# One output store before a crossbar transpose moves from the sync queue to GpSimd's queue

## The chip, the cores and the metric

The kernel runs on one core of one Trainium2 chip. The metric is the device time of one execution in microseconds. The three runs of the kernel before took 199.21, 198.86 and 199.10 us; their median is 199.1 us. Engines are called as in the profile: PE is TensorE's matmul, PEld its weight load, DVE is VectorE, ACT is ScalarE, POOL is GpSimd, SP is SyncE, which computes nothing and issues transfers. A "q" behind a name (SPq, POOLq) means the queue of that engine.

## The reference

The kernel computes the time-mixing part of an RWKV layer for 16 batches of 2048 tokens with 256 channels, float32 in and out. Each token is mixed with its predecessor by a weight per channel, the mix goes through two projections, one of them through a sigmoid, and the product of both goes through the output projection. The reference also computes a third projection, k, which the output doesn't use.

```python
x_prev[:, 1:, :] = x[:, :-1, :]
xv = x * time_mix_v + x_prev * (1 - time_mix_v)
xr = x * time_mix_r + x_prev * (1 - time_mix_r)
v = xv.reshape(-1, d_model) @ value_weight
r = xr.reshape(-1, d_model) @ receptance_weight
out = (1.0 / (1.0 + np.exp(-r)) * v).reshape(-1, d_model) @ output_weight
```

## The kernel before, in words

**Units.** A batch of 2048 tokens is cut into 4 units of 512 tokens, so there are 64 units (NU), and unit u belongs to batch u // 4. The main loop (line 646) runs once per unit g; its last unit is done by last_unit. The multiplication by time_mix is folded into the weights (w_bf), so mixing is "scale the token by a coefficient, then add its predecessor".

**One step g of the loop**, in the order of the program: TensorE projects unit g with the receptance weight into the accumulator psum_r (project, line 384); ScalarE takes the sigmoid (line 658); transfers and transposes for later units are issued (advance, and the block at line 660); from g=33 on ScalarE copies the output of unit g-2 out of its accumulator and stores it (output, line 471 and store, line 437), earlier steps do this at the end for unit g-1; the mix of coming units is made: VectorE scales one half of the channels (line 354), GpSimd the other half (scale_pool, line 364), from step 34 on ScalarE does some of VectorE's scales (line 638), and VectorE adds the predecessors (add, line 376); TensorE projects the unit with the value weight into psum_v, of which there is one buffer; VectorE multiplies it with the sigmoid into z_sb (line 697); GpSimd's scale for a later pair of units follows. A pair of units shares one scale of GpSimd: the one in step g=39 is for units 42 and 43, first mix, and the one in g=40 is for their second mix. VectorE adds to the first mix of unit 42 right behind the product of g=40, and to its second mix at the start of g=41.

**Two ways to transpose the input.** The projections need channels on the partitions, so the input is transposed. Batches 0 to 9 are loaded as bfloat16 by GpSimd's queue into x_bf and transposed by TensorE (line 272). Batches 10 to 15 (STAGED = 10 and up) go another way: GpSimd's queue loads them, cast to bfloat16, from HBM into a scratch tensor in HBM, x_natural (load, lines 158 and 162), and one DMA transpose by the crossbar for each group of three batches, issued by SP, brings them into xt_both (by_dma, line 254). T_AT = {27: 10, 39: 13} says in which step: batches 10 to 12 in step 27, batches 13 to 15 in step 39. The loads of batches 13, 14 and 15 are issued in steps 33, 34 and 35 (STAGE_AT), held back until the first transpose has landed. Batch 15 is loaded in two halves (HALVED), so loads[15] has two transfers; by_dma waits for the second, called whole in the loop. In by_dma and store, `after=` adds a wait for a transfer to the instruction issued.

**Stores.** The outputs of two units make one store of 1 MB. Stores are issued by SP, in order; some pairs are not stored at once. FIRST = {19: 27, 21: 27, 27: 39} names pairs (by their second unit) that are held until a step with a transpose and stored ahead of it, after the first half of the group's last load (half) has landed. WAITING names pairs that are held until the same step and stored behind the transpose: for step 39, those of units 29, 31, 33 and 35. Step 39 thus has one store ahead of the transpose, that of units 26 and 27, and four behind it. The first five lines of the loop that decide this are:

```python
if g in T_AT:
    half, whole = loads[T_AT[g] + 2]
    for pair in firsts.pop(g):
        store(nc.sync, *pair, after=half)
    last_t = by_dma(T_AT[g], whole)
```

**Queues.** Instructions of one engine run in the order of the program, and an instruction that waits holds up what is behind it on its engine. GpSimd's instructions around step 39 are: the loads of batches 13 to 15 (steps 33 to 35), and one scale of line 364 in each step. SP's are the stores and the transpose.

Of the kernel before, what the change touches and what calls it, by code (L numbers as in the profile page):

```python
# [15 lines left out]
def kernel(  # L16
# [25 lines left out]
    nc = tc.nc  # L42
# [18 lines left out]
    T_AT = {27: 10, 39: 13}  # L61
# [330 lines left out]
    def project_unmixed(ps, mo):  # L392


        parts = [(w_prev[:, ko], ko, 0) for ko in range(KO)]
        parts += [(w_bf[:, 0, ko], ko, 1) for ko in range(KO)]
        for n, (w, ko, lo) in enumerate(parts):
            nc.tensor.matmul(
                out=ps[:, mo, :],
                lhsT=w[:, mo * P : (mo + 1) * P],  # L400
                rhs=xt[0][:, lo : lo + UJ, ko],
                start=(n == 0),
                stop=(n == len(parts) - 1),
            )
# [19 lines left out]
    def store(queue, b, lo, hi, after=None):  # L424
        src = o_sb[b, lo // (2 * UJ)]
        j = lo % (2 * UJ)
        src = src[:, j : j + hi - lo, :]
        if b < STAGED:
            dst = out[b].rearrange("(p j) d -> p j d", p=P)[:, lo:hi, :]
        elif b in STAGED_PAIRS:  # L430
            h = lo // (2 * UJ)
            dst = out[b, h * 2 * TU : (h + 1) * 2 * TU].rearrange("(p j) d -> p j d", p=P)[:, j : j + hi - lo]
        else:
            n = min(hi - lo, UJ)
            dst = out[b, lo * P : hi * P].rearrange("(e p j) d -> p e j d", p=P, j=n)
            src = src.rearrange("p (e j) d -> p e j d", j=n)
        op = queue.dma_start(out=dst, in_=src)
        if after is not None:
            tc.add_manual_dep(op.ins, after.ins.name, SYNC, reason="in turn with the last load")
# [93 lines left out]
    def pieces(g):  # L533

        b, e = divmod(g, UB)
        tile_for(g // 2)
        return [(b, m, e * TU, (e + 1) * TU) for m in range(2)]

    def wrap_slots(piece, one=None, after=None):


        b, _, lo, _ = piece
        by_unit = b < BYUNIT
        key = (b, lo // TU if by_unit else UB - 1)
        if key not in late_copies:
            return
        kos = slice(0, KO) if one is None else slice(one, one + 1)
        if one in (None, KO - 1):
            late_copies.remove(key)
        j = slots(piece).start if by_unit else 0  # L550
        n = UJ if by_unit else J
        if by_unit and j > 0:
            engine = nc.vector if key == (0, 1) else nc.gpsimd
            engine.tensor_copy(out=xt[b][:, j, kos, 0:1], in_=xt[b][:, j - 1, kos, P - 1 : P])
        if key in shifted:
            return
        op = (nc.vector if after is None else nc.gpsimd).tensor_copy(  # L557
            out=xt[b][:, j, kos, 1:P], in_=xt[b][:, j + n, kos, 0 : P - 1]
        )
        if after is not None:  # L560
            tc.add_manual_dep(op.ins, after.ins.name, SYNC, reason="one at a time")
# [4 lines left out]
    def advance(limit):  # L566
        nonlocal tnext
        while tnext <= min(limit, NU - 1):
            b, e = divmod(tnext, UB)
            for n in LOADS.get((b, e), ()):  # L570
                loads[n] = load(n)
            if tnext < NU - BYDMA:
                transposes(tnext)
            tnext += 1
# [71 lines left out]
    for g in range(NU - 1):  # L646
        ps_r = ps_r_pool.tile([P, KO, TU], FP32, name="psum_r")
        if g == 0:
            project_unmixed(ps_r, 0)
            advance(1)  # L650
            project_unmixed(ps_r, 1)
            wrap_slots(pieces(1)[0])
            scale(pieces(1)[0])
            last = add(pieces(1)[0])
        else:
            project(ps_r, g, 0)
        s_sb = zpool.tile([P, KO, TU], BF16, name="s_sb")
        nc.scalar.activation(out=s_sb, in_=ps_r, func=ACT.Sigmoid)  # L658
        advance(START_T[g] if g < len(START_T) else g + LOOK)
        if g in T_AT:  # L660
            half, whole = loads[T_AT[g] + 2]
            for pair in firsts.pop(g):
                store(nc.sync, *pair, after=half)
            last_t = by_dma(T_AT[g], whole)
            for pair in kept.pop(g, []):
                store(nc.sync, *pair)
        if LATE_O < g < NU - 2:
            output(g - 2, z_prev2)
        for p in products.get(g + 1, []):
            if g >= FREE and p[0][1] == 1:  # L670
                scale_act(p[0], (0,))
        for p in [q for q, _ in products[g]] + pooled[g]:
            last_unit_of = p[3] // TU - 1
            need = last_unit_of if p[0] < BYUNIT else min(last_unit_of + 1, UB - 1)
            assert UB * p[0] + need < tnext, (g, p, tnext)
            if g > AHEAD or p not in pooled[g]:
                wrap_slots(p)
        if g == 1:
            load(2)
            scale_act(pieces(2)[1], (1,))  # L680
        for p, kos in products[g]:
            if not (g - 1 >= FREE and p[1] == 1):
                scale(p, kos)
        for p in sums[g]:
            last = add(p)
        for p in pooled[g]:
            if p[0] >= BYUNIT:
                wrap_slots(p)
        ps_v = ps_v_pool.tile([P, KO, TU], FP32, name="psum_v")
        project(ps_v, g, 1)  # L690
        if g == 0:
            scale_act(pieces(1)[1], (0,))
            advance(2)
        z_sb = zpool.tile([P, KO, TU], BF16, name="z_sb")
        n = TU // 2 if g == NU - 2 else TU
        for c in range(0, TU, n):
            nc.vector.tensor_tensor(  # L697
                out=z_sb[:, :, c : c + n],
                in0=s_sb[:, :, c : c + n],
                in1=ps_v[:, :, c : c + n],  # L700
                op=ALU.mult,
            )
        for p in pooled[g]:
            wrap_slots(p, after=last)
            scale_pool(p, last)
        if ZEROS_AT <= g < ZEROS_AT + len(pads):
            zero_rows(*pads[g - ZEROS_AT])
        if g in STAGE_AT:
            b = STAGE_AT[g]
            loads[b] = load(b)  # L710
            for op in loads[b] if b in HALVED else [loads[b]]:
                tc.add_manual_dep(op.ins, last_t.ins.name, SYNC, reason="not beside transposes")
        for p in held[g]:
            add(p)
        if z_prev is not None and not LATE_O <= g < NU - 3:
            output(g - 1, z_prev)
        z_prev2, z_prev = z_prev, z_sb
# [31 lines left out]
```

## Time and profile before

| what | before |
|---|---|
| median of three runs | 199.1 us (198.86 to 199.21) |
| span of the profiled execution | 197.1 us |
| time of the runs outside the span (median less span) | 2.0 us |
| mean granted clock of TensorE | 0.996 |
| HBM read, written | 34.34 MB, 39.90 MB |
| first transpose: issue, landing | 95.38 us, 18.8 us later |
| second transpose: issue, landing | 133.86 us, 15.7 us later |

The profile is of one execution of its own, for which the span is given and no other time. It shows busy time by engine, the chain of work that ended last, groups of instructions by line, and the transfers. In a row of a line, "x1: 333/333/333, 131.3 to 131.3" gives the count, the shortest, median and longest duration in ns, and the first and last start in us. "DMA to landing" is the time from a transfer's issue to its completion. In a timeline a row gives start, duration, engine, line, operation, output<-input, and in brackets the engine's idle time before it with what ended it. In a table of stretches come the stretch, its length, the busy times of PE, PEld, DVE, ACT and POOL with their counts, the granted clock, the busy share of the 16 DMA engines (values over 1 come from overlapping packets) and the GB/s that they moved. Matmul ends are modelled, so neighbouring rows of PE overlap by a little.

### The profile page before, as it was taken

To read this page: it belongs to the slowest core of one execution; us is meant where nothing else is said; L and a number is where in the kernel's file an instruction comes from. 1 tells how busy PE (TensorE), PEld (TensorE's weight loads), DVE (VectorE), ACT (ScalarE), POOL (GpSimd) and SP (SyncE) were. 2 spreads that over 40 slices of the span, in tenths; PEclk is the share of its full clock that TensorE was granted. 3 is DMA by queue.
4 is the path that set the end of the run, shared out by engine and by line. 5 is a ranking of instruction groups with operands and counts; after the bars stand their busy time and mean duration, and the time that the engine had idled before them with its cause. 6 is when DMAs were issued, how large, how long until landed. Compare 5 with 4: busy or idle time off the path is not lost.

```text
span 197.1 us, 3735 instructions
## 1 busy us (share of the span) xinstructions
PE 191.5 (97%) x1358; PEld 123.0 (62%) x1364; DVE 183.1 (93%) x286; ACT 177.1 (90%) x197; POOL 86.3 (44%) x117
## 2 busy tenths in 40 slices
PE   8999999999999999999999999999999999999992
PEld 3556676666666666666666666666666666666660
DVE  0999999999999999999999999999999999999962
ACT  3699899999999999999999999999999999999982
POOL 2845542443665635624334266444433444444200
PEclk9999999999999999999999999999999999999998
DMA  5999999999999999999999999999999999999985
GB/s 185 238 176 224 218 254 262 247 259 262 296 413 283 283 296 332 283 238 198 376 209 290 335 346 186 212 218 241 290 290 419 419 421 419 416 416 421 382 327 221
DMA packets 35593, 58.13 MB, mean 295 GB/s; under 512 B 26004, under 2 KB 27128, under 8 KB 30840
## 3 DMA queue, kind: packets, MB, share of 16 engines
q1 hardware_dynamic: 31792, 41.34, 60.3%
q0 software_dynamic: 3632, 16.44, 41.6%
q8 instruction: 10, 0.16, 0.3%
q10 hardware_dynamic: 152, 0.13, 0.2%
q14 instruction: 7, 0.06, 0.1%
HBM read 34.34 MB, written 39.90 MB: 377 GB/s over the span
## 4 chain that ended last, share of the span: by engine, by line
PE 90%; DMA 6%; POOL 1%; issue 0%; SPq 0%; ACT 0%
PE psum_r L384 27%; PE psum_v L384 27%; PE psum_o L416 27%; PE ps_t L272 8%; DMA x_bf<-in_x_dram 4%; DMA w_f<-n_receptance_weight_dram 2%; PE ps_t L416 1%; POOL x_bf L192 1%; SPq L174 0%; POOL wo_bf L195 0%; PE psum_v L416 0%; POOL x_bf L152 0%; PE ps_t L384 0%; PE psum_r L416 0%; ACT x_bf L446 0%
## 5 line engine op out<-in xcount | busy, mean ns | idle before, releaser
L364 POOL TENSOR_SCALAR mix<-xt_both,c_sb 128x1024 bf16<-128x1024 bf16 (+1 forms) x55 | 61.1, 1110 | 85.5 <-DVE mix L376 82.3
L697 DVE TENSOR_TENSOR z_sb<-s_sb,psum_v 128x1024 bf16<-128x1024 bf16 (+1 forms) x64 | 76.8, 1201 | 2.3 <-PE psum_v L384 1.1
L376 DVE TENSOR_TENSOR mix<-mix,xt_both 128x1024 bf16<-128x1024 bf16 x112 | 76.8, 696 | 1.4
L384 PEld LDWEIGHTS <-w_bf 128*128 128x128 bf16 x512 | 48.5, 98 | 39.2 <-DVE mix L376 0.8
L658 ACT ACTIVATE s_sb<-psum_r 128x1024 bf16<-128x1024 f32 x63 | 65.2, 1034 | 6.2 <-PE psum_r L384 6.0
L384 PE MATMUL psum_v<-mix,w_bf 128*128 128x512 bf16 (+1 forms) x252 | 64.8, 378 | 0.4 <-DVE mix L376 0.2
L384 PE MATMUL psum_r<-mix,w_bf 128*128 128x512 bf16 x250 | 64.6, 379 | 0.2
L416 PE MATMUL psum_o<-wo_bf,z_sb 128*128 128x256 bf16 x486 | 63.2, 273 | 0.0
L416 PEld LDWEIGHTS <-z_sb 128*128 128x128 bf16 x512 | 52.0, 103 | 17.9 <-DVE z_sb L510 0.7
L471 ACT COPY o_sb<-psum_o 128x1024 f32<-128x1024 f32 x50 | 51.2, 1023 | 5.0 <-PE psum_o L416 4.8
L289 ACT COPY xt_both<-ps_t 128x1024 bf16<-128x1024 bf16 x32 | 32.9, 1039 | 0.0
L272 PEld LDWEIGHTS <-x_bf 128*128 128x128 bf16 x304 | 19.8, 98 | 8.4 <-DMA x_bf<-in_x_dram 0.4
L272 PE MATMUL ps_t<-ident,x_bf 128*128 128x128 bf16 x304 | 22.7, 219 | 0.2 <-DMA x_bf<-in_x_dram 0.2
L354 DVE TENSOR_SCALAR mix<-xt_both,c_sb 128x1024 bf16<-128x1024 bf16 (+1 forms) x47 | 21.3, 463 | 0.0
L638 ACT ACTIVATE mix<-xt_both,c_sb 128x1024 bf16<-128x1024 bf16 x14 | 16.3, 1163 | 0.0
L376 DVE TENSOR_TENSOR mix<-mix,xt_first 128x1024 bf16<-128x1024 bf16 x15 | 10.5, 708 | 0.1
L471 ACT COPY x_bf<-psum_o 128x1024 f32<-128x1024 f32 x10 | 10.2, 1015 | 0.0
L354 DVE TENSOR_SCALAR mix<-xt_first,c_sb 128x512 bf16<-128x512 bf16 x22 | 6.6, 350 | 0.3 <-ACT xt_first L282 0.2
L289 ACT COPY xt_first<-ps_t 128x1024 bf16<-128x1024 bf16 x6 | 6.0, 1022 | 0.0
L557 POOL COPY xt_first<-xt_first 128x254 bf16<-128x254 bf16 x5 | 2.0, 392 | 7.2 <-DVE mix L376 7.2
L162 POOL DMA_DIRECT2D x_bf<-in_x_dram x8 | 4.7, 584 | 0.0
L364 POOL TENSOR_SCALAR mix<-xt_first,c_sb 128x512 bf16<-128x512 bf16 x6 | 4.1, 685 | 1.3 <-DVE mix L376 0.8
(68 smaller groups left out, 52.3 us busy)
## 6 DMA issues: line engine op xcount, KB each, us to landing
out_dram<-o_sb SPq DMA_DIRECT2D x25, 1024.0 KB, 12.1
x_bf<-in_x_dram POOLq DMA_DIRECT2D x8, 1024.0 KB, 15.8
x_natural<-in_x_dram POOLq DMA_DIRECT2D x4, 1024.0 KB, 11.8
out_dram<-x_bf SPq DMA_DIRECT2D x4, 1024.0 KB, 14.4
x_natural<-in_x_dram POOLq DMA_DIRECT2D x4, 512.0 KB, 12.7
out_dram<-x_bf SPq DMA_DIRECT2D x4, 512.0 KB, 4.7
x_bf<-in_x_dram POOLq DMA_DIRECT2D x6, 256.0 KB, 7.0
o_sb<-in_x_dram SPq DMA_DIRECT2D x4, 256.0 KB, 3.9
```

What stands on the lines that cost most here:

```text
L162: return nc.gpsimd.dma_start(out=x_bf[b], in_=rows(b), max_dma_last_dim=run)
L272: nc.tensor.transpose(out=ps[:, jj], in_=src[:, jj, ko * P : (ko + 1) * P], identity=idn)
L289: nc.scalar.copy(out=xt[b][:, j0 : j0 + UJ], in_=ps)
L354: nc.vector.tensor_scalar(out=mixed(piece, ko), in0=tokens(piece, 0, ko), scalar1=c_sb[:, m, ko : ko + 1], scalar2=None, op0=ALU.mult,)
L364: op = nc.gpsimd.tensor_scalar(out=mixed(piece, 1), in0=tokens(piece, 0, 1), scalar1=c_sb[:, m, 1:2], scalar2=1.0, op0=ALU.mult, op1=ALU.mult,
L376: return nc.vector.tensor_tensor(out=mixed(piece), in0=mixed(piece), in1=tokens(piece, 1), op=ALU.add)
L384: nc.tensor.matmul(out=ps[:, mo, :], lhsT=w_bf[:, m, ko, mo * P : (mo + 1) * P], rhs=mixed((b, m, e * TU + lo, e * TU + hi), ko), start=(k ...
L416: nc.tensor.matmul(out=ps[:, j, :], lhsT=slot[:, ko, j], rhs=wo_bf[:, ko, :], start=(ko == 0), stop=(ko == KO - 1),)
L471: nc.scalar.copy(out=o[:, j0 : j0 + UJ, :], in_=ps)
L638: nc.scalar.activation(out=mixed(piece, ko), in_=tokens(piece, 0, ko), func=ACT.Copy, scale=c_sb[:, m, ko : ko + 1],)
L658: nc.scalar.activation(out=s_sb, in_=ps_r, func=ACT.Sigmoid)
L697: nc.vector.tensor_tensor(out=z_sb[:, :, c : c + n], in0=s_sb[:, :, c : c + n], in1=ps_v[:, :, c : c + n], op=ALU.mult,)
```

## The change

In the step of the last transpose (max(T_AT) is 39) the held store is issued by GpSimd instead of SP, and it is given no wait for the half load. The store ahead of the first transpose, in step 27, stays as it is. In step 39 this concerns one store, that of units 26 and 27.

```diff
         if g in T_AT:
             half, whole = loads[T_AT[g] + 2]
             for pair in firsts.pop(g):
-                store(nc.sync, *pair, after=half)
+                if g == max(T_AT):
+                    store(nc.gpsimd, *pair)
+                else:
+                    store(nc.sync, *pair, after=half)
             last_t = by_dma(T_AT[g], whole)
             for pair in kept.pop(g, []):
                 store(nc.sync, *pair)
```

## The prediction

> **What bounds the kernel now.** I read the page's busy times and chain first, to learn which engine sets the end; then a table of stretches around the change; then TensorE's timeline there; last, one by one, the moved store, the loads and transpose that it stands between, and GpSimd's queue, which it is moved to.
>
> ```profile
> span 197.1 us, 3735 instructions
> PE 191.5 (97%) x1358; PEld 123.0 (62%) x1364; DVE 183.1 (93%) x286; ACT 177.1 (90%) x197; POOL 86.3 (44%) x117
> PE 90%; DMA 6%; POOL 1%; issue 0%; SPq 0%; ACT 0%
> ```
>
> TensorE carries 90% of the chain that ended last; the 6% of DMA is the first weight and input. The span is 197.1 us and the median of the runs is 199.1, so 2.0 us lie outside the span, and I sum against 197.1 + 2.0. Differences of up to about 0.2% (0.4 us) can't be told from no change by this kernel's measurement.
>
> Two views of the stretch around the change: a table (length, then busy time with count for PE, PEld, DVE, ACT, POOL, then granted clock, DMA share and GB/s), and four lines of TensorE's timeline.
>
> ```profile
> 120.00:128.60 8.60, 8.60 (x54) 5.03 (x53) 8.60 (x13) 8.19 (x10) 4.18 (x5) 1.00 1.01 209
> 138.00:146.70 8.70, 8.65 (x53) 5.49 (x54) 8.68 (x14) 7.88 (x9) 3.48 (x4) 1.00 1.27 290
> 148.00:186.00 38.00, 37.84 (x234) 24.35 (x235) 37.88 (x52) 35.13 (x38) 16.20 (x15) 1.00 1.02 419
> ```
> ```profile
> 113.86 1.03 PE L416 MATMUL psum_o<-wo_bf,z_sb 128*128 128x256 bf16 x8
> 129.46 1.04 PE L416 MATMUL psum_o<-wo_bf,z_sb 128*128 128x256 bf16 x8
> 133.79 1.03 PE L384 MATMUL psum_r<-mix,w_bf 128*128 128x512 bf16 x4
> 135.53 1.03 PE L384 MATMUL psum_v<-mix,w_bf 128*128 128x512 bf16 x4
> ```
>
> The DMA engines are busy all the time too, but at very different rates: 209 GB/s while the last staged loads run, 290 during the transpose, 419 once only stores are left. None of that shows on TensorE. Six units lie between the two psum_o rows, (129.46 - 113.86) / 6 = 2.60 us each, with the clock at 1.00. So a change of DMA order is worth something only if it makes TensorE, or an engine that feeds it, wait.
>
> **What is removed from SP.** Rows of line 437 around the store, then of line 254, the transpose.
>
> ```profile
> L437 SPq EVENT_SEMAPHORE  x1: 19557/19557/19557, 111.7 to 111.7; - x1
> L437 SPq DMA_DIRECT2D out_dram<-o_sb x1: 333/333/333, 131.3 to 131.3; - x1
> DMA to landing us min/median/max: 6.5/6.5/6.5
> ```
> ```profile
> SPq L254 <- DMA x_natural<-in_x_dram: 2.0, 1, 2.0
> L254 SPq DMA_TRANSPOSE xt_both<-x_natural x1: 12865/12865/12865, 133.9 to 133.9; - x1
> DMA to landing us min/median/max: 15.7/15.7/15.7
> ```
> ```profile
> L162 POOL DMA_DIRECT2D x_natural<-in_x_dram x1: 562/562/562, 114.7 to 114.7; - x1
> DMA to landing us min/median/max: 9.1/9.1/9.1
> ...
> L162 POOL DMA_DIRECT2D x_natural<-in_x_dram x1: 552/552/552, 117.3 to 117.3; - x1
> DMA to landing us min/median/max: 11.3/11.3/11.3
> L158 POOL DMA_DIRECT2D x_natural<-in_x_dram x2: 544/553/562, 119.7 to 120.3; - x2
> DMA to landing us min/median/max: 11.5/12.5/13.4
> ```
>
> SP waits 19.6 us for the first half of the last load, issues the store at 131.3 in 0.33 us, waits 2.0 us more for the second half and issues the transpose at 133.9. Without the store SP waits once, for the second half. Is that half earlier now? Load 14 landed at 117.3 + 11.3 = 128.6, the halves of load 15 at 119.7 + 11.5 = 131.2 and 120.3 + 13.4 = 133.7: steps of 2.6 and 2.5 us. The second half, with the store issued beside its end, took no longer than the first. Removing the store from in front gives the transpose 0 us; the 0.33 us of issue lay inside SP's wait. Nothing else of SP is queued in that time: the next stores in its program stand behind the transpose.
>
> **What is added on GpSimd.** Its timeline, and VectorE's beside it.
>
> ```profile
> 119.72 1.10 POOL L158 DMA_DIRECT2D x_natural<-in_x_dram  x2
> 126.58 1.12 POOL L364 TENSOR_SCALAR mix<-xt_both,c_sb 128x1024 bf16<-128x1024 bf16 x1 [1.63 <-DVE mix L376]
> 129.01 1.12 POOL L364 TENSOR_SCALAR mix<-xt_both,c_sb 128x1024 bf16<-128x1024 bf16 x1 [1.30 <-DVE mix L376]
> 131.78 1.12 POOL L364 TENSOR_SCALAR mix<-xt_both,c_sb 128x1024 bf16<-128x1024 bf16 x1 [1.66 <-DVE mix L376]
> 155.00 1.12 POOL L364 TENSOR_SCALAR mix<-xt_both,c_sb 128x1024 bf16<-128x1024 bf16 x1 [1.30 <-PE psum_v L384]
> ```
> ```profile
> 131.00 0.69 DVE L376 TENSOR_TENSOR mix<-mix,xt_both 128x1024 bf16<-128x1024 bf16 x1
> 132.73 1.31 DVE L376 TENSOR_TENSOR mix<-mix,xt_both 128x1024 bf16<-128x1024 bf16 x2
> 134.06 1.22 DVE L697 TENSOR_TENSOR z_sb<-s_sb,psum_v 128x1024 bf16<-128x1024 bf16 x1
> ```
>
> The two issues at 119.72 belong to loop step g=35; one scale (line 364) follows per step, so those at 126.58, 129.01 and 131.78 are of g=38, 39 and 40. In program order the store stands between the first two: GpSimd reaches it at 126.58 + 1.12 = 127.70 and has nothing to do until 129.01. One issue costs 0.55 us (544 to 562 ns above), so it is hidden in 1.31 us of idling: 0 us. What it writes out, unit 27's pair, was copied some ten steps earlier, so its data keep it from nothing.
>
> If that cover were gone: the scale of g=39 is first needed by VectorE at 132.73, that of g=40 (ready for start at 131.69) by the second add there, at 132.73 + 0.65 = 133.38. Without delay g=40's ends at 131.78 + 1.12 = 132.90, 0.48 us early. The scale of g=39 may thus start as late as 133.38 - 2 x 1.12 = 131.14, 3.44 us after 127.70. From there VectorE waits; its product at 134.06 ends 135.28 and frees the accumulator that TensorE writes at 135.53, so 0.25 us later TensorE waits too. The issue costs nothing up to 3.7 us.
>
> **What moves among transfers.** The moved megabyte no longer runs ahead of the transpose in SP's queue, but behind the loads in GpSimd's. The rate in 40 slices of 0.225 us from 131 to 140 us, and the tail in stretches:
>
> ```profile
> GB/s 237 182 200 237 218 146 310 310 200 455 473 328 400 510 437 218 437 364 182 217 196 192 174 57 97 73 46 0 15 114 291 291 290 290 291 290 290 289 291 288
> 186.00:189.00 3.00, 3.00 (x22) 2.06 (x21) 2.68 (x5) 2.53 (x4) 0.00 (x0) 1.00 0.87 354
> 189.00:192.00 3.00, 3.00 (x24) 2.12 (x22) 1.76 (x3) 2.74 (x6) 0.00 (x0) 1.00 0.70 281
> ```
>
> The loads' 200 GB/s turn into the store's 400 or so at about 132.4; the store's bytes are through by 135.05 (slice 18). Twelve slices with a mean of 114 GB/s follow until the transpose reaches 290, just when the store lands (131.3 + 6.5 = 137.8): 2.7 us at 114 / 290, a start-up loss of 1.6 us. In the new order the store's bytes follow the last load's on the same engines, so again from about 132.4; the transpose is issued at 133.9 as before. Its cost is not in the trace; the bounds are that the start-up loss disappears (1.6 us gained for the transfers) or doubles (1.6 lost). I take 0, since total bytes and starting times stay.
>
> What would either bound be worth? The transposed data land at 133.9 + 15.7 = 149.6 and GpSimd reads them first at 155.00 (g=49, batch 13): 5.4 us to spare. The stores behind the transpose keep the DMA engines full to about 186; in the last two rows they idle 3 x 0.13 + 3 x 0.30 = 1.3 us before the last stores are issued. So 1.6 us lost delays the end by 0.3 us, and 1.6 us gained enters a queue whose end waits for TensorE: 0 us.
>
> Sum: SP 0 + GpSimd 0 + transfers 0 (0 to +0.3) = 197.1 + 2.0 = 199.1 us.
>
> **The rivals.** *GpSimd is held by the issue* (slower). It waits at the store for room in its queue, or to write the descriptors, until load 15 has landed at 133.7. The scales of g=39 and 40 then end at 134.8 and 135.9, the add at 133.38 starts 2.6 us late, and 2.6 - 0.25 = 2.3 us reach TensorE, which has no idle time to win back: 201.4. It decides from 3.7 us of holding. Against it: at 119.72 the two halves of load 15 were issued at 0.55 us each while loads 13 (landed at 114.7 + 9.1 = 123.8) and 14 were still on their way; load 14, load 15 and the store, outstanding at 127.70, are as many bytes. The Trainium skill, SBUF — State Buffer, section "A bandwidth-pool intuition that's wrong (but worth ruling out)", speaks against this change: GpSimd can't write descriptors while VectorE holds their shared port, and a DMA of about 620 ns took about 3100 ns so. By that figure the sum would still be 199.1 (an estimate), with 0.3 us left to the point where VectorE waits; the issues of 0.54 to 0.56 us beside a VectorE busy 8.60 of 8.60 us don't show such a lock. Chance 0.05.
>
> *Store and transpose in turns* (slower). If the two queues share each engine, the store's 2.7 us of bytes (132.4 to 135.05) take up to twice as long, it lands 2.7 us later, and the transpose gets to its full rate only then: 2.7 - 1.3 of idle tail = 1.4 us, 200.5. It decides from 1.3 + 0.4 = 1.7 us of lost DMA time. For it: full rate came just at the store's landing. Against it: the engines can do the transpose's work while the store waits. The Trainium skill, DMA: Bandwidth & Descriptors, section "Queues, rings and completion order", says that an engine serves its queues in turn, a packet at a time; that is this mechanism, and the trace of before, with both in one queue, can't show it. Chance 0.08.
>
> *The store overtakes the loads.* If it ran beside load 15 from 127.7 on, the second half would land up to 2.5 us later and the transposed data at 152.1, still before 155.00; the bytes are the same, so 199.1. It belongs to the forecast's case.
>
> *Faster.* An earlier transpose helps only what waits for it, and nothing does. What could shrink is the landing of the last store.
>
> ```profile
> 193.79 0.38 ACTq L437 DMA_DIRECT2D out_dram<-x_bf  x1
> DMA to landing us min/median/max: 2.1/2.2/2.3
> ```
>
> From 2.3 to 2.1 us, 198.9 at best. Chance of more than 0.4 us: 0.07, for what I overlook.
>
> **How the numbers follow.** No measurable change 0.80 (forecast and overtaking store), held issue 0.05, turns 0.08, faster 0.07; slower is 0.05 + 0.08 = 0.13. The middle case spans 198.7 to 199.5 (0.4 us to each side, which holds the +0.3 bound); to leave out less than 2 in 10 I stretch it a little into the slower cases: 198.7 to 199.7.
>
> **What would show it.** Right: one issue of line 437 on GpSimd near 127.7, about 0.55 us; the scale of g=39 still near 129.0; SP's wait from 111.7 on ending with the second half instead of the first; the transpose issued near 133.9; TensorE at 2.60 us per unit through 140 us and no new wait of ACT for buffers. Wrong: the scale of g=39 after 131, the transposed data landing after 155, or DMA share at 1.0 up to 192.

## The result: about 0.6% slower, because more of the executions end late

Over 20 runs each, taken in turns, the kernel after had a median of 200.77 us (198.88 to 201.65) against 199.31 us (198.86 to 202.18) before. The ratio of after to before is 1.0059, with a 95% interval of 1.0034 to 1.0084. The ratios of this document leave out executions over 1.5% above the fastest of their kernel (here 202.18 and 201.90 us before), so they aren't those of the medians (1.0073 here). The forecast of no measurable change was wrong, and 200.77 lies outside its range.

The medians hide how it is slower. With the runs of the experiments below, there are 66 times of the changed program and 160 of the one before. Neither has one hump:

```
               times  median   at most 200.0            over 200.0
before           160  199.20   138, median 199.2        22 (14%), median 200.7
after             66  200.67    26, median 199.4        40 (61%), median 201.0
```

The change moves the early group by about 0.3 us, and makes the late group, about 1.6 us behind, four times as frequent. The execution whose profile came with the result is one of the early ones (199.09 us), so what is lost has to be looked for in other executions too. First that profile: its span, busy times and chain.

```profile
span 197.3 us, 3735 instructions
PE 192.0 (97%) x1358; PEld 123.2 (62%) x1364; DVE 183.3 (93%) x286; ACT 177.3 (90%) x197; POOL 86.7 (44%) x118
PE 92%; DMA 2%; DVE 2%; SPq 1%; issue 1%; POOL 0%; ACT 0%; DVEq 0%; POOLq 0%
```

One instruction more on POOL, the other counts alike. GpSimd's timeline around the new issue:

```profile
126.73 1.12 POOL L364 TENSOR_SCALAR mix<-xt_both,c_sb 128x1024 bf16<-128x1024 bf16 x1 [1.63 <-DVE mix L376]
127.79 0.60 POOL L437 DMA_DIRECT2D out_dram<-o_sb  x1
129.16 1.11 POOL L364 TENSOR_SCALAR mix<-xt_both,c_sb 128x1024 bf16<-128x1024 bf16 x1 [0.77 <-DVE mix L376]
```

The issue takes 0.60 us and lies wholly in the idle time ahead of the scale of g=39, of which 0.77 us are left. The scale starts at 129.16 instead of 129.01, with the whole program 0.2 us later from its start. Next the last load's halves (line 158), then the transpose (line 254):

```profile
L158 POOL DMA_DIRECT2D x_natural<-in_x_dram x2: 544/554/563, 119.9 to 120.4; - x2
DMA to landing us min/median/max: 11.6/12.8/14.0
```
```profile
L254 SPq DMA_TRANSPOSE xt_both<-x_natural x1: 12619/12619/12619, 134.6 to 134.6; - x1
DMA to landing us min/median/max: 15.5/15.5/15.5
```

The halves land at 131.5 and 134.4, 2.95 us apart (14.0 - 11.6 + 0.55 between the issues); before it was 2.45 by the same sum. So the transpose is issued at 134.6 instead of 133.9 and its data land at 150.1 instead of 149.6, still 5 us ahead of their first use. The rate from 131 to 140 us, in the same 40 slices as the prediction's row, shows the load's last stretch:

```profile
GB/s 255 182 127 164 182 200 182 73 200 200 346 364 455 364 400 510 400 400 364 583 255 219 130 124 108 159 154 32 56 175 86 238 287 290 289 291 275 287 290 282
```

Ten slices at a mean of 176 GB/s come ahead of the store's 400, where before there were six at 203. The end, though, looks as before:

```profile
186.00:189.00 3.00, 3.00 (x22) 2.06 (x21) 2.68 (x5) 2.68 (x4) 0.00 (x0) 1.00 0.96 388
189.00:192.00 3.00, 3.00 (x26) 2.26 (x23) 1.79 (x3) 2.60 (x6) 0.00 (x0) 1.00 0.72 294
```

The DMA share rises from 0.87 to 0.96 in the first stretch and is 0.72 instead of 0.70 in the second: in this execution the delay is swallowed before the end.

### The profile page after: what moved, and what is told of

Same layout as the page of the kernel before. It is cut to its first block, busy times and chain, and to the rows that moved or that the text cites. A ratio compares the mean times of both kernels' runs of the same rounds, so it can differ in the third digit from the quotient of the medians.

```text
span 197.3 us, 3735 instructions
## 1 busy us (share of the span) xinstructions
PE 192.0 (97%) x1358; PEld 123.2 (62%) x1364; DVE 183.3 (93%) x286; ACT 177.3 (90%) x197; POOL 86.7 (44%) x118
## 4 chain that ended last, share of the span: by engine, by line
PE 92%; DMA 2%; DVE 2%; SPq 1%; issue 1%; POOL 0%; ACT 0%; DVEq 0%; POOLq 0%
PE psum_v L384 27%; PE psum_r L384 27%; PE psum_o L416 27%; PE ps_t L272 8%; DMA w_f<-in_value_weight_dram 2%; PE ps_t L416 1%; SPq L174 1%; DVE mix L376 1%; DVE mix L354 0%; DVE w_bf L594 0%; POOL mix L364 0%; PE psum_v L416 0%; SPq L180 0%; PE ps_t L384 0%; PE psum_r L416 0%
```

## The late executions, and where their time goes

*h2_again* and *h3_again* are one execution each of the unaltered change; both fell among the late ones (200.74 and 200.42 us). The views of h2_again that answer to those above: the load's halves, the transpose, and the stretches.

```profile
L158 POOL DMA_DIRECT2D x_natural<-in_x_dram x2: 547/554/562, 119.8 to 120.4; - x2
DMA to landing us min/median/max: 12.0/13.5/15.1
```
```profile
L254 SPq DMA_TRANSPOSE xt_both<-x_natural x1: 12608/12608/12608, 135.6 to 135.6; - x1
DMA to landing us min/median/max: 15.4/15.4/15.4
```
```profile
186.00:189.00 3.00, 3.00 (x22) 2.06 (x21) 2.68 (x5) 2.64 (x4) 0.00 (x0) 1.00 1.00 414
189.00:192.00 3.00, 3.00 (x25) 2.22 (x23) 1.80 (x3) 2.64 (x6) 0.00 (x0) 1.00 0.97 393
```

The halves are 3.65 us apart, the transpose is issued at 135.6, and at the end the DMA share is 1.00 and 0.97: the sign that the prediction named for a wrong forecast. TensorE is not late. Its first psum_r matmuls of line 384 and its last ones, from its timeline:

```profile
10.56 1.04 PE L384 MATMUL psum_r<-mix,w_bf 128*128 128x512 bf16 x4
...
189.37 1.03 PE L384 MATMUL psum_r<-mix,w_bf 128*128 128x512 bf16 x4
```

That is 178.81 us of work, against 178.90 in the same two rows before:

```profile
10.37 1.04 PE L384 MATMUL psum_r<-mix,w_bf 128*128 128x512 bf16 x4
...
189.27 1.03 PE L384 MATMUL psum_r<-mix,w_bf 128*128 128x512 bf16 x4
```

The span of 199.0 is 10.56 + 178.81 + 9.63; before it was 10.37 + 178.90 + 7.83. All of it but the start's 0.19 is the tail behind the last unit, 1.80 us longer, because the last stores land late. The clock is no rival here: in every profile but that of e4_pool_wait it was granted at 1.00 from 6.8 us or sooner until more than a microsecond behind the last matmul, and at 0.50 from there on. A longer tail alone thus lowers the mean clock of an execution (0.993 in the change's late times, 0.998 in its early ones). The landings:

```profile
DMA to landing us min/median/max: 3.8/3.9/4.0
```

Before they took 2.1 to 2.3. Why they land late is seen at the transpose's other end. The rate from 146 to 156 us, in slices of 0.25 us, first before and then in h2_again:

```profile
GB/s 289 293 290 290 290 292 288 290 640 525 164 360 524 492 492 393 197 524 525 459 328 328 459 524 459 328 328 459 525 492 262 393 426 524 492 262 426 393 525 426
```
```profile
GB/s 292 292 287 292 291 290 289 292 288 291 291 315 269 127 14 8 8 685 360 164 524 524 524 492 131 426 524 525 492 262 295 524 492 524 524 66 492 492 524 524
```

Before, the stores behind the transpose (over 400 GB/s) follow its 290 at 148.0 without a pause. In the late execution the transpose runs to 149.25 and then some 8 GB/s trickle for about 0.9 us, a hole, before the stores start. By the transfers' records, the seventeenth store packet (some of the first sixteen come early in some runs) starts at 150.71 instead of 148.42; with the program's start 0.2 us later that is 2.1 us late, the hole's 0.9 included.

How that passes the idle time that the prediction counted on, the transfers' own records tell. This is the number of packets under way, as a mean over each 0.25 us from 184 us on (there are 16 DMA engines; the records don't name them, and one packet under way is taken for one engine at work):

```
before     16 16 16 16 16 16 16 16 16 16 16 10  3 10 16 16 16 16 16 16 16 16 16 14  3  3  2  2 14 16 16 16 16 15 16 15  3 13 16 14  6 16 16 16 16 16  9  0
after      16 16 16 16 16 16 16 16 16 16 16 16 16 11 14 16 16 16 16 16 16 16 16 16 10  3  3  3  7 16 16 16 16 15 16 16 11  5 16 16  9 11 16 17 16 16 16  4  0
h2_again   16 16 16 16 16 16 16 16 16 16 16 16 16 16 16 16 16 17 16 16 16 16 17 16 16 16 16 15 10 16 16 16 16 16 16 16  9  8 16 16  8 14 16 17 16 16 15  4  3  2  1  1  1  1  0
```

Before, the pauses near 187 and 190 are not pauses of all engines: one to three still work, and are through at 190.95, when the next stores come. The engines don't keep step, and the pause lets the laggards catch up. In the late execution the pause is gone, the stores follow each other without it, and the laggards' arrears stand at the end: one to four engines work on for 1.75 us when the others have finished.

The Trainium skill, DMA: Bandwidth & Descriptors, section "Latency and other measured facts", says that two of the sixteen engines are usually slower; these records show up to four that lag, and not which.

No execution of the change above 200.8 us was profiled, and 21 of its 40 late times lie above 201.0. In two profiles of other programs that do (e2_behind at 201.66 and c1_copy at 201.97 us, below) TensorE's work took 179.79 and 180.09 us, about 1 us longer than here, beside a long tail (9.6 and 9.2 us). So the slowest executions may lose a second microsecond elsewhere; this stays open.

## The experiments

All but h2_again and h3_again were timed in turns with the kernel before on the same chip. In the accounts below, "late" means over 200.0 us. The first theory was that the store, once it no longer waits, slows the load in front of it in its queue, so that the transpose and then the end are late. The rivals were the prediction's (held GpSimd, turns) and that it isn't the moved store at all, but the program's layout, its start, or the measurement.

**The same programs again.** *e1_again*, *f3_again* and *f4_again* are the change, unaltered.

> The changed kernel once more, unaltered, to see an execution that is slow and not only the one at 199.09 us that was profiled. Its 20 runs lie between 198.9 and 201.7 us, so something comes and goes from one execution to the next. Theory A (transposed data late): store and transpose share the engines, in most executions the second transpose lands after GpSimd wants its data (155 us), TensorE stalls once at about 155 to 160 us, and the granted clock may fall for some us after it; median 200.5 to 201. Theory B (clock alone): no wait is longer than before, and the clock is below 1.00 in some stretch that no wait precedes. Theory C (held issue): in slow executions the issue of the store on GpSimd takes over 3.7 us instead of 0.60. The forecast's own reading, that nothing changes: 199.1 to 199.5.

> The changed kernel with a blank line at its end, for another profile of one execution, hopefully slow. Theory T: in a slow execution the second half of load 15 lands more than 2.5 us behind the first, the second transpose reaches its full rate after 138.5 us, and the last transfer takes 3 us or more from issue to landing; TensorE within 0.3 us of the kernel before plus its start. Theory S: last transfer 2.1 to 2.3 us as before, TensorE late from the start. Median 200.2 to 200.8.

> The same once more, with two blank lines at its end; expectations as for the run ahead of it.

Ratios 1.0040 (1.0009 to 1.0072), 1.0043 (1.0009 to 1.0078) and 1.0039 (1.0008 to 1.0069); 5, 6 and 5 of 12 times late. It repeats on two chips, and each time as a mixture. All three profiled executions are early ones (200.00, 199.55 and 198.83 us), with the load's halves 3.65, 3.45 and 3.05 us apart. *c1_copy* is the kernel before, run as if it were the change, and *c2_lines* has only three blank lines added:

> The kernel before, unaltered, run as if it were a changed one, beside the kernel before. In the traces so far all of a longer span lies in the first 11 us: the first weight lands between 3.6 us (kernel before) and 5.1 us after its issue, and from the first main projection to the last the changed kernel takes 178.8 us against 178.9. Theory D (start, not the change): how long the first loads take varies from execution to execution whatever the program, and the changed kernel only had an unlucky share; this copy then spreads from 198.9 to 201.8 like the changed one, median 199.5 to 200.3. Theory E (the program's own effect on its start): the copy stays as tight as the kernel before, median 199.2, at most 3 of 20 runs over 200.

> The kernel before with three blank lines put where the change has its three more; the instructions are the same to the byte. A second draw of the copy: theory D 199.5 to 200.3 with a spread to 201.8; theory E 199.2 and tight.

0.9998 (0.9981 to 1.0015) with 2 of 12 late, and 1.0027 (1.0001 to 1.0052) with 3 of 12. The second is a warning: the same instructions can give 0.3% and an interval that just misses 1. (c1_copy's profile, of an execution of 201.97 us, isn't compared below, since its TensorE lost 1.2 us as well. So no late execution of the kernel before was read that lost time in its tail alone.) *c3_oneline* has the change's instructions without its extra lines, *c4_spot* has the kernel before with one more tiny instruction on GpSimd at step 39:

```diff
-                store(nc.sync, *pair, after=half)
+                store(*((nc.gpsimd, *pair) if g == max(T_AT) else (nc.sync, *pair, half)))
```
```diff
-            half, whole = loads[T_AT[g] + 2]
+            half, whole = loads[T_AT[g] + 2]; nc.gpsimd.memset(zeros[:, 0:1], 0.0) if g == 39 else None
```

> The changed kernel written without additional lines; its instructions are those of the changed kernel. Theory D: the same spread as the copy of the kernel before in this call, median 199.5 to 200.3. Theory E: median 200 to 200.8 while the copy stays at 199.2.

> The kernel before with one small instruction more on GpSimd in step 39 (a memset of one zero column that holds zero already); the store stays on SP. GpSimd's program gets as long as in the changed kernel, while the store isn't moved. Theory D: as the copy. Theory E by the length of the program: spreads like the changed kernel, 200 to 200.8; theory E by the store: tight, 199.2.

1.0092 (1.0061 to 1.0123) with 7 of 8 late, and 1.0004 (0.9982 to 1.0027) with 2 of 12. So the cost follows the moved store, not lines, layout or one more instruction.

**Queue and wait apart.** *e2_behind* puts the store behind the transpose in SP's queue; *e3_sp_nowait* leaves it on SP without the wait; *e4_pool_wait* has it on GpSimd with the wait.

```diff
-                store(nc.sync, *pair, after=half)
+                if g != max(T_AT):
+                    store(nc.sync, *pair, after=half)
+                else:
+                    kept[g].insert(0, pair)              # e2_behind
+                store(nc.sync, *pair)                    # e3_sp_nowait, in step 39
+                store(nc.gpsimd, *pair, after=half)      # e4_pool_wait, in step 39
```

> The store is put behind the second transpose, on SP, as the first of the stores kept for that step; nothing stands ahead of the transpose any more and no store shares the engines with it. Theory A: the transposed data land earlier than in either kernel, so median 199.1 or a little less and less spread than before. Theory B: clock dips as often as in the kernel before, 199.3. Theory C: no issue on GpSimd, so as before, 199.3. If the tail of stores is what decides (1.3 us idle at the end), 2.5 us of store added behind the transpose would give up to 200.5.

> The store stays on SP's queue ahead of the transpose, only its wait for the half load is taken away: it is issued right behind the two stores of the step 27, at about 112 us, and has landed before the loads of batches 13 to 15 are half done. Tells the wait apart from the queue. Theory A: the transpose has no store beside it at all, 199.1; loads at most 2.5 us later. Theory B: as before, 199.3. Theory C: as before, 199.3.

> The store on GpSimd's queue, but with the wait for the half load, so GpSimd stands still from 127.8 to about 131.4 us and the scale of step 39 starts at about 132 instead of 129.2. It prices a held GpSimd (theory C): by the prediction's margin of 3.7 us, the hold of 3.6 + 0.6 us gives TensorE a wait of about 0.5 us, so at least 199.6, and a stall near 133 to 136 us. Theory A: the store's bytes come no earlier than in the changed kernel, so the same late data in addition, 200.5 to 201.5.

e2_behind: 1.0040 (1.0012 to 1.0068), 9 of 12 late, though four of them by less than 0.1 us. With no store ahead of the transpose the kernel gains nothing; the time is that of the expectation's last sentence. e3_sp_nowait: 1.0057 (1.0028 to 1.0086), 7 of 12; SP issues the store at 111.6, it runs ahead of the loads of batches 13 to 15, and both halves land some 2 us later than before, 2.45 apart. None of the expected times (199.1 to 199.3) came true. e4_pool_wait: 1.0077 (1.0052 to 1.0103), 6 of 6. Here GpSimd does stand still, and the price of that can be read; its waits in 118 to 150 us, then TensorE's psum_r rows:

```profile
POOL out_dram L437 <- DVE mix L354: 3.4, 1, 3.4
```
```profile
133.44 1.03 PE L384 MATMUL psum_r<-mix,w_bf 128*128 128x512 bf16 x4
136.82 1.04 PE L384 MATMUL psum_r<-mix,w_bf 128*128 128x512 bf16 x4 [0.62 <-DVE mix L376]
139.44 1.03 PE L384 MATMUL psum_r<-mix,w_bf 128*128 128x512 bf16 x4
142.24 1.03 PE L384 MATMUL psum_r<-mix,w_bf 128*128 128x512 bf16 x4
```

A hold of 3.4 us for the wait (the view names another releaser; by the time it is the half load) and the issue behind it cost TensorE 3.38 - 2.60 = 0.78 us at once and 0.20 later. That is the prediction's rival of the held GpSimd, deciding a little sooner than where it was put (4.0 us of holding less 3.7 would have cost 0.3); the change itself shows nothing of the kind. The 0.98 us are about half of the 1.9 by which the median rose; the rest isn't accounted for. (The profiled execution, 202.23 us, started late too, with its first psum_r at 12.64 and the clock granted at 0.50 from 6.9 to 10.3 us.) And with the wait the halves are 2.45 us apart again (landing after 11.1 and 13.0 us, issued 0.55 apart), while in all eight profiles with the change's store (the cut one below among them) they are 2.75 to 3.65 apart. One profile with the wait, g3_late_transpose below, has 2.75 too; the others with it have at most 2.55. Dropping the wait slows the load.

**Does it go through the end?** *f1_after_drop* is the change and *f2_before_drop* the kernel before, both with two of the kept stores cut out, 2 MB less behind the transpose.

```diff
-            for pair in kept.pop(g, []):
+            for pair in kept.pop(g, [])[: 2 if g == 39 else None]:
```

> The changed kernel without two of the four stores behind the second transpose (those of units 33 and 35, so 2 MB of the output are not written). The slow execution traced so far (200.77 us) has TensorE 0.1 us behind the kernel before, but its last transfer lands 1.8 us later: the DMA engines are late after the second transpose and don't catch up. Theory T (the tail): the order of store, load and transpose puts the transfers behind by more than the 1.3 us that they idle before the end; with 2 MB (5 us) less behind the transpose that can't reach the end, so median 199.0 to 199.3, as tight as the same cut of the kernel before. Theory S (the start): the longer executions come from later first loads or another wait of TensorE; then 200.2 to 200.8, as before the cut.

> The same cut of the kernel before (the stores of units 33 and 35 left out), as the other side of the comparison. Theory T and theory S: 198.9 to 199.2; a little under the kernel before where its own slower executions came from the tail.

199.80 us (199.46 to 200.17) and 199.16 us (199.04 to 199.73); against the uncut kernel before, 1.0014 (0.9990 to 1.0037) and 0.9992 (0.9972 to 1.0013). The group near 201 us is gone in both. By the transfers' records all engines now stand still for 1.26 and 0.91 us before the end, so laggards are caught up. The late group's delay reaches the end through the stores behind the transpose: shown. But f1 is still 0.6 us above f2, and in its profile this part doesn't take that path, since all engines had stood still until 191.3. There the last stores landed in 2.0 to 2.9 us instead of 2.1 to 2.3, and one packet at a time, that of a single laggard, was under way for the last 0.45 us. An 8 KB packet of an instruction queue had taken 0.46 us at 194.49, behind the issue of the last store; in f2 it came at 193.49, ahead of it. Whether this packet is the cause wasn't tried.

**The moment, the queue, the transpose alone.** *g1_late40* and *g2_late41* issue the store on GpSimd one and two steps later, *h1_act41* issues it on ScalarE's queue where g2 had it, and *g3_late_transpose* is the kernel before, but for a transpose that waits until the store has landed.

```diff
+                    late = pair                      # g1, g2, h1: kept in step 39
...
+        if g == 41:                                  # 40 in g1
+            store(nc.gpsimd, *late)                  # nc.scalar in h1
```
```diff
-                store(nc.sync, *pair, after=half)
-            last_t = by_dma(T_AT[g], whole)
+                landed = store(nc.sync, *pair, after=half)
+            last_t = by_dma(T_AT[g], landed if g == max(T_AT) else whole)
```

> The store is issued by GpSimd without a wait, but one loop step later: GpSimd reaches that place behind the scale of g=39, at about 130.2 us, some 1 us before the first half of the last load lands (131.2). Theory (a store that stands in GpSimd's queue behind the last load slows that load's second half; the transpose starts later, and the DMA engines don't win it back before the end): the second half lands 2.45 to 2.8 us behind the first instead of 2.85 to 3.65, because the store is queued for 1 us less of the load's time than 3.5; the time lies between before and the change, 199.2 to 199.8. Rival (GpSimd's queue is worse for this store at any moment, since it shares the engines in turns with the transpose): as slow as the change, 200.0 to 200.8, with halves 2.45 us apart.

> As the run before, two loop steps later than in the change: GpSimd reaches the store at about 132.9, 1.7 us after the first half has landed and 0.8 us before the second one. Theory: halves 2.45 us apart, the transpose issued at 133.9 to 134.3, and the time of before, 199.2 (within 0.4). Rival (GpSimd's queue at any moment): halves 2.45 us apart, and still 200.0 to 200.8. If the store, coming 1.6 us later than in the kernel before, leaves the DMA engines idle behind the loads, both give up to 0.3 us more.

> The kernel before, with its store on SP and its wait, but the transpose waits until that store has landed (137.8) instead of for the last load: it is issued at about 138.2, 4.3 us later than in the profile before (133.9), and its data land at about 153.8, still ahead of the first read at 155.0. Theory (a late transpose costs DMA time that the 1.3 us of idling ahead of the last stores don't cover): the store's bytes end at about 135.1 and the transpose is at its full rate 2.7 us behind its issue, at 140.9 instead of 137.8; 3.1 us more at about 114 of 290 GB/s lost make 1.9 to 3.1 us, less 1.3 of idling: 0.6 to 1.8 us slower, 199.8 to 201.0, with the last stores landing in over 3 us instead of 2.2. Rival (nothing that happens to the transposes reaches the end, as the prediction had it with its 0.3 us): 199.2 to 199.5, last stores landing in 2.2 us.

> The store goes out on ScalarE's queue, without a wait, at the step at which the run with the store two steps later had it on GpSimd's: ScalarE gets there behind its sigmoid of g=41, at about 133.4 us; its issue of 0.38 us lies in front of an idle 0.41 us at 134.4 and should cost nothing. If GpSimd's queue is what costs (loads and store in one queue): the profile and time of before, 199.2 to 199.5, and transposed data in at most 138.1 us behind the first psum_r. If it costs that the store's bytes are no longer between the loads and the transpose, on whichever queue: as the run two steps later, 200.0 to 200.6, with the DMA engines idle for about 1 us ahead of the store and the first stores behind the transpose over 139 us behind the first psum_r.

g1: 200.80 us, 1.0048 (1.0017 to 1.0078), 11 of 12 late, halves 2.95 apart: as slow as the change, where the theory wanted less. g2: median 200.35, 1.0018 (0.9981 to 1.0056), 7 of 12 late; by the ratio it can't be told from before. Its profiled execution is a late one, and for this one the theory in its first form isn't enough. The load is undisturbed and the transpose is issued at 133.9, as before, and yet:

```profile
L254 SPq DMA_TRANSPOSE xt_both<-x_natural x1: 14348/14348/14348, 133.9 to 133.9; - x1
DMA to landing us min/median/max: 17.1/17.1/17.1
```

The transpose takes 1.5 us longer to issue and 1.4 longer to land, and the end is late (200.66 us in the profiled execution). The rate from 131 to 140 us shows why:

```profile
GB/s 182 255 273 164 182 255 164 109 127 18 73 0 0 510 291 328 546 400 291 400 364 182 109 218 182 73 146 218 291 3 122 278 246 36 13 160 287 290 291 289
```

The load's bytes are through at about 133.3, the store, issued at 132.84, brings nothing until 133.9, and its bytes run where the transpose would begin. h1 issues the store on ScalarE's queue at 132.63, which is 0.7 us earlier in the program, since its first psum_r comes at 10.90 instead of 10.45; there the store's bytes follow the load's without a hole:

```profile
GB/s 164 273 237 200 164 255 218 218 182 218 146 310 401 364 400 546 255 400 437 400 255 255 218 255 146 36 75 166 264 166 14 15 167 290 291 290 289 291 291 289
```

h1: 199.37 us, 1.0012 (0.9982 to 1.0042), 4 of 12 late; by its ratio it can't be told from before, nor from g2. The two profiles suggest that it isn't enough to keep the load free, and that the store must also come in time to fill the stretch between the load and the transpose; with one profile each that is argued, not shown. The store landed 127.5 us behind the first psum_r in h1, 128.7 in g2, and 127.4 both before and in the change. Whether GpSimd's queue is worse as such isn't separated by this pair, which differs in the moment too. (h1's expectation wanted the transposed data by 138.1 and missed: they landed at 139.7, and at 139.2 before. The first stores behind them started at 138.5.) The Trainium skill, DMA: Bandwidth & Descriptors, section "Issuing engines are not separate DMA queues", says that issuing from several engines only saves the issuing sequencer's time. No sequencer time was at stake here, and yet the same store gave medians of 199.2 (SP, with the wait), 199.4 (ScalarE) and 199.8 to 201.1 (GpSimd, three moments). At the first two of these moments the loss is clear of the noise, so the place of this transfer did matter.

g3: 201.67 us, 1.0086 (1.0049 to 1.0124), 11 of 12 late, about the most that was expected by the ratio (1.7 us) and more by the median. The store and the loads are as before within 0.3 us, only the transpose is late:

```profile
L254 SPq DMA_TRANSPOSE xt_both<-x_natural x1: 11322/11322/11322, 137.7 to 137.7; - x1
DMA to landing us min/median/max: 14.1/14.1/14.1
```

Issued 3.8 us later it lands 2.2 us later, at 151.8, over 3 us ahead of its first use; and the kernel is 2.5 us slower by its median (201.67 - 199.21). A late transpose by itself costs: shown. The last two are the late executions read above:

> The change, unaltered, one look. Theory: in a quick execution (below 199.6) the first stores behind the transpose start at most 138.8 us behind the first psum_r and the last stores land in 2.1 to 2.5 us; in one of over 200.3 they start over 139.5 us behind it, with the DMA engines nearly idle for about 1 us behind the transpose, and the last stores land in 3.5 to 4.3 us. Rival (the late executions lose their time elsewhere, in the start or on TensorE): both look alike here.

> The same kernel and the same two outcomes as in the run before; with two looks the chance that neither is one of the late executions is about a quarter.

The first stores behind the transpose start 140.15 and 140.00 us behind the first psum_r (early executions of the change: 138.3 to 138.6), and the last stores land in 3.8 to 4.0 and 3.5 to 3.8 us. As the theory had it; the rival of a late start or a late TensorE falls for these two.

**One order for all.** The table puts the profiles in order of the time at which SP has issued the whole transpose (its start and duration in the row of line 254), counted from the first psum_r. "Halves" is how far apart the load's halves land; "lands" is the transposed data, counted likewise; "slowest slice" is the lowest rate in a slice of 0.25 us from 146 to 153 us; the tail goes from the last psum_r to the end of the span. Halves, landings and tails are worked out from rounded rows and hold to about 0.1 us.

```
                   halves  transpose issued..done  lands  slowest slice       last stores  tail
f2_before_drop      2.55      123.3 .. 135.6       138.5   66 GB/s                    2.1-2.3     7.95
c4_spot             2.45      123.5 .. 135.8       138.6   174                        2.1-2.3     7.79
c2_lines            2.45      123.7 .. 136.0       138.8   229                        2.1-2.5     7.80
before              2.45      123.5 .. 136.4       139.2   164                        2.1-2.3     7.83
after               2.95      124.0 .. 136.6       139.5   164                        2.1-2.3     7.89
f3_again            3.45      124.5 .. 136.7       139.5   131                        2.1-2.5     7.92
h1_act41            2.45      123.5 .. 136.9       139.7   229                        2.2-2.5     7.96
f4_again            3.05      123.9 .. 136.9       139.8   229                        2.1-2.4     8.01
e1_again            3.65      125.0 .. 137.0       139.8   179                        2.3-2.5     7.98
e4_pool_wait        2.45      123.1 .. 137.0       139.9   46                         2.1-3.0     7.98
e3_sp_nowait        2.45      125.4 .. 137.1       139.9   131                        2.3-2.6     8.02
g1_late40           2.95      123.7 .. 137.2       140.1   7                          3.5-3.7     9.21
h3_again            3.45      124.5 .. 137.5       140.3   8                          3.5-3.8     9.32
c3_oneline          2.75      124.3 .. 137.6       140.5   7                          3.9-4.0     9.62
h2_again            3.65      125.0 .. 137.7       140.4   8                          3.8-4.0     9.63
g2_late41           2.45      123.5 .. 137.8       140.6   7                          3.9-4.0     9.65
g3_late_transpose   2.75      126.9 .. 138.2       141.0   7                          4.1-4.5     9.88
```

Whatever made the transpose late, up to 137.1 us the tail stays within 7.8 to 8.0, and from 137.2 on it is over 9.2: a step, not a slope. (Left out are f1, which lacks 2 MB, with its transpose done at 136.9 and a tail of 8.6, and e2, which has 1 MB more behind its transpose, done at 137.2, a tail of 9.6, and a TensorE that took 0.9 us longer.) The kernel before (with its store as it is: the first four rows) stands 0.7 to 1.5 us ahead of the step, the change on it: 136.6 to 137.7. The halves alone don't place an execution; 3.65 us occurs on both sides.

## Why the prediction was wrong, by its own steps

*GpSimd: right.* One issue at 127.79, 0.60 us long, 0.77 us of idle time left. The rival of the held GpSimd fell; e4_pool_wait shows what it would have looked like.

*TensorE: right.* It needed 178.65 to 178.83 us from the first psum_r to the last in all eight profiles with the change's store, against 178.90 before, and waited for nothing new.

*"The second half, with the store issued beside its end, took no longer than the first. Removing the store from in front gives the transpose 0 us": this step failed.* It took the two steps of 2.5 and 2.6 us for proof that a store beside the load's end is harmless, but that store was issued at 131.3, when the half load had just landed; the new one is queued at 127.8, some 3.5 us before that. The load's second half then lands 0.3 to 1.2 us later behind the first.

*"I take 0, since total bytes and starting times stay": it failed with that.* The bytes stayed. The transpose was issued 0.4 to 1.6 us later, counted from the first psum_r.

*The bounds of the transfers: mis-sized.* Lost time of up to 1.6 us was inside the prediction's bound, and priced at 1.6 - 1.3 = 0.3 us, by the 1.3 us that the DMA engines idle before the end. Measured in h2_again: a first store that comes 2.1 us later makes the tail 1.8 us longer. The 1.3 us are a mean over 16 engines; one to three of them work through those pauses. Idle share is no slack where the slowest engine has none.

*Store and transpose in turns* (200.5, chance 0.08) came out near in time, with lost DMA time as its price and a point from which it decides. That is a coincidence, since the mechanism was another: the store wasn't stretched by 2.7 us. In the first profile it was issued at 127.8 and landed 10.2 us later, at 138.0, against 137.8 before, both 127.4 behind the first psum_r; in the three late profiles of the change it landed at 127.9 to 128.3. By the rule of the Trainium skill, DMA: Bandwidth & Descriptors, section "Queues, rings and completion order" (an engine serves its queues in turn), it could have been; these traces don't show it.

*Not settled:* why the engines trickle at 8 GB/s for a microsecond behind a late transpose; what decides within one program on which side of the step an execution falls; how a queued store slows load packets in front of it; f1's last 0.6 us; what the executions above 201 us lose besides. None of the variants is faster than the kernel before.

## What to carry to other kernels

A wait in front of a transfer can be useful work: it kept the store out of the load's way and let it fill the time until the transpose started. Before counting DMA idle time as slack, count how many engines idle: a share of 0.7 can be thirteen engines waiting for three. And where a kernel ends in stores, the median may move by how often a step is crossed; then the early profile shows nothing, and one has to profile executions until a late one is there.

## What the runs showed of the hardware

- A store queued without a wait behind a load in GpSimd's queue slows the load before its own first byte moves: by the transfers' records the load's 4 KB packets took 338 to 398 ns on the mean up to that moment in the eight profiles with the change's store, and 324 to 337 ns in six profiles in which the store waits for the half. Queued 2.5 us later (g1_late40) it left them at 333 ns.
- The transpose's first packet follows 1.3 us behind its issue, and its full rate of 290 GB/s 2.4 to 3.1 us behind it when nothing else runs (e2_behind, e3_sp_nowait, g3_late_transpose). Part of the "start-up loss" of 1.6 us in the prediction is that, whatever stands in front.
- In all the profiles behind the step of the table an 8 KB packet of an instruction queue is served 1.1 us or more before the transpose has ended (at 148.88 us in h2_again, 1.6 us ahead of its last packet); in all those ahead of it, it comes within 0.3 us of the end. Whether it is cause or sign of the hole wasn't tried.
